# Two thirds of the down projection by Strassen's scheme, one weight pool, and the last 256 tokens written token-major

## The chip, the cores and the metric

The kernel runs on one core of a Trainium2 chip. The metric is the device time of one execution in microseconds (us). A TensorE matmul keeps a 128x128 stationary tile in the array and streams up to 512 columns past it. VectorE (DVE in the profile), ScalarE (ACT), GpSimd (POOL) and SyncE (SP) each run their instructions in their program's order; SP, ACT and POOL also start DMA transfers.

## The reference, cut to what matters

Two layers over 512 tokens of width 1024, all float32. The second half of each layer is the convolutional feed-forward network (FFN), with `D_FF` = 2816; the first half is a mixing block that the change leaves as it is.

```python
def conv_ffn(h, w_up, conv_w, conv_b, w_down):
    up = h @ w_up                                   # 1024 -> 2 x 2816
    s_len = up.shape[1]
    padded = jnp.pad(up, ((0, 0), (CONV_WIDTH - 1, 0), (0, 0)))
    conv = conv_b + padded[:, 0:s_len] * conv_w[0]
    for j in range(1, CONV_WIDTH):
        conv = conv + padded[:, j:j + s_len] * conv_w[j]
    gate, val = jnp.split(conv, 2, axis=-1)
    return (jax.nn.silu(gate) * val) @ w_down       # 2816 -> 1024

    for l in range(DEPTH):
        ...
        x = x + conv_ffn(rms_norm(x, norm2_g[l]), w_up[l], conv_w[l], conv_b[l], w_down[l])
    return rms_norm(x, final_g)
```

## The kernel before

Activations lie with channels on the partitions and the 512 tokens along the free axis: `X` is eight tiles of 128x512. Every large product is taken in three matmuls (`mm3`, line 217): each float32 operand is split into a rounded part (hi, type float32r) and the remainder (lo), and hi·hi, hi·lo and lo·hi are added up in one PSUM bank.

Weights come in slots of 512 KB (128 partitions x 1024 values), 96 per layer, in the order of use. `Weights._emit` (line 81) loads one slot into a raw tile by a DMA on SP's queue, ACT makes the hi tile (line 87) and DVE the lo tile (line 88). There are three pools of five tiles (raw, hi, lo). `get(s)` asks for slots up to `s + LOOK`, that is three ahead.

The FFN (`ffn`, line 591) goes in two halves of 11 channel blocks (`FH`). For each block j two up projections (`proj`, line 223: 8 x 3 matmuls of 512 columns) fill a bank each, one for the gate and one for the value; DVE scales each out of PSUM (line 611), ACT and DVE do the convolution (lines 613 and 617), ACT the SiLU (line 621), DVE the product (line 623), and `split` (line 119) makes the hi and lo tiles of G. After 11 blocks the down projection of the half runs: eight output tiles m, each 11 x 3 matmuls of 512 columns in one bank (`dn`), and one DVE addition into `X[m]` (line 633).

The last half of layer 1 is `finish` (line 640). Its first six output tiles are as above (`fd`); for the last two (`FIN` = 2) the left 256 tokens and then the right 256 tokens are done apart, with matmuls of 256 columns. The squares of `X` are summed, `fin_stats` (line 679) reduces them over the partitions by matmuls (`fss`) and `rsqrt` takes a chain of small DVE and ACT steps; `fin_out` (line 693) spreads the result over the partitions by matmuls with the identity (`frb`) and scales the eight tiles on DVE (line 703) before the output DMAs. The left half's `fin_out` stands among the right half's matmuls, the right half's at the very end.

Within this program text a scheduler (the Tile framework) fixes each engine's order and the semaphores that it waits on, from its own estimates of durations; a tile of a pool can be taken anew only when the last reader of its previous content is done, and that too becomes a wait.

Of the kernel before, what the change touches and what calls it, by code (L numbers as in the profile page):

```python
# [29 lines left out]
NHALF = 2  # L30
FH = FT // NHALF
# [22 lines left out]

class Weights:
    def __init__(self, tc, ctx, wflat):
        self.nc = tc.nc
        self.w = wflat
        self.raw_pool = ctx.enter_context(tc.tile_pool(name="wraw", bufs=5))
        self.hi_pool = ctx.enter_context(tc.tile_pool(name="whi", bufs=LOOK + 2))  # L60
        self.lo_pool = ctx.enter_context(tc.tile_pool(name="wlo", bufs=LOOK + 2))
        self.n = DEPTH * SLOTS_PER_LAYER
        self.next = 0
        self.slots = {}

    def first(self, load_x):
        nc = self.nc
        for s in range(4):
            raw = self.raw_pool.tile([P, 2, T], F32, tag="raw", name=f"wr{s}")
            hi = self.hi_pool.tile([P, 2, T], F32R, tag="hi", name=f"wh{s}")  # L70
            lo = self.lo_pool.tile([P, 2, T], F32R, tag="lo", name=f"wl{s}")
# [28 lines left out]
def trunk(ctx: ExitStack, tc: tile.TileContext, xT, wflat, vec, ws_t, bias_t, bw, rope, dmask, vdec, geps, cnt, sel, out):  # L100
# [3 lines left out]
    up = ctx.enter_context(tc.tile_pool(name="units", bufs=48))  # L104
# [21 lines left out]
    X = []  # L126
# [463 lines left out]

    def ffn(l, nm, nxt):
        base = l * SLOTS_PER_LAYER + 30
        vc = l * LC
        hs, ls = nm.h, nm.l
        s = base
        up_ps = [proj(f"up{l}_0_0", s, hs, ls)]
        nm.stats()
        up_ps.append(proj(f"up{l}_0_1", s + 1, hs, ls))
        nm.spread()
        for hf in range(NHALF):  # L600
            G = []
            for j in range(hf * FH, hf * FH + FH):
                c2 = []
                for which in range(2):
                    n = f"{l}_{j}_{which}"
                    ps = up_ps.pop(0) if up_ps else proj("up" + n, s, hs, ls)
                    s += 1
                    t = which * FT + j
                    w = [vecs[:, vc + C_CW + i * 2 * FT + t : vc + C_CW + i * 2 * FT + t + 1] for i in range(3)]
                    u = U("uu" + n)  # L610
                    nc.vector.tensor_tensor(out=u, in0=ps, in1=nm.bc, op=ALU.mult)  # L611
                    c = U("cc" + n)
                    nc.scalar.activation(  # L613
                        out=c, in_=u, func=AF.Identity, scale=w[2], bias=vecs[:, vc + C_CB + t : vc + C_CB + t + 1]
                    )
                    for d in (1, 2):
                        nc.vector.scalar_tensor_tensor(  # L617
                            out=c[:, d:], in0=u[:, : T - d], scalar=w[2 - d], in1=c[:, d:], op0=ALU.mult, op1=ALU.add
                        )
                    if which == 0:  # L620
                        nc.scalar.activation(out=c, in_=c, func=AF.Silu)  # L621
                    c2.append(c)
                nc.vector.tensor_tensor(out=c2[0], in0=c2[0], in1=c2[1], op=ALU.mult)
                G.append(split(c2[0], f"G{l}_{j}"))
            if nxt is None and hf == NHALF - 1:
                finish(s, G)
                return
            for m in range(KT):
                ps = PS(f"dn{l}_{hf}_{m}")
                for k in range(FH):  # L630
                    i = m * FH + k
                    mm3(ps, W.get(s + i // KT), i % KT, G[k][0], G[k][1], k == 0, k == FH - 1)
                nc.vector.tensor_tensor(out=X[m], in0=X[m], in1=ps, op=ALU.add)  # L633
                if hf == NHALF - 1:
                    nxt.feed(m)
            s += FH
# [202 lines left out]
```

## Time and profile before

| | us |
|---|---|
| median of 3 runs (lowest, highest) | 1140.11 (1140.07, 1140.3) |
| the profiled execution, its own time | 1139.73 |
| its span, first to last instruction | 1138.0 |
| PE busy (matmuls), 5387 instructions | 1128.0 (99%) |
| DVE busy, 1104 instructions | 746.7 (66%) |
| ACT busy, 731 instructions | 525.3 (46%) |

The profiled execution's own time is 1.7 us over its span, for what lies before the first and after the last instruction. Matmuls are pipelined: a 128x512 matmul is shown with some 390 ns, but the next one starts well before it ends, so that what a matmul costs is read from the distance of starts and not from its duration. PEclk is the share of full clock that TensorE was granted.

### The profile page before, as it was taken

What the parts mean: (1) busy time and instruction counts of PE and PEld (TensorE: products, weight loads), DVE (VectorE), ACT (ScalarE), POOL (GpSimd) and SP (SyncE); (2) the same over time, 40 slices, a digit from 0 to 9 for tenths busy, and PEclk for the clock granted to TensorE, in tenths of its full rate; (3) what the DMA queues carried; (4) which work ended last, traced back from release to release, by engine and by line L of the source; (5) the groups of instructions that cost most, each with busy time, mean ns of one, the idle gap of its engine ahead of it and who ended that gap; (6) DMA issues with size and microseconds to landing.
All of it is one profiled execution on the core that took longest, in us unless ns stands there. A gap on an engine that the chain in (4) does not pass through costs nothing.

```text
span 1138.0 us, 13734 instructions
## 1 busy us (share of the span) xinstructions
PE 1128.0 (99%) x5387; PEld 942.3 (83%) x5387; DVE 746.7 (66%) x1104; ACT 525.3 (46%) x731; POOL 27.4 (2%) x71
## 2 busy tenths in 40 slices
PE   9999999999999999999999999999999999999997
PEld 7888888888888888888888898888888888888886
DVE  6998776577753377774448877666777425777534
ACT  7677735444431244444327785534444213444420
POOL 2010000000000000000001000000000000000000
PEclk9999999999999999999999999999999999999999
DMA  9432223232233222333224322222332223222202
GB/s 328 144 117 88 75 75 109 77 111 93 93 96 107 94 93 93 105 99 111 93 93 129 94 77 72 75 95 91 99 105 93 93 95 108 94 93 93 93 1 74
DMA packets 33362, 112.83 MB, mean 99 GB/s; under 512 B 4321, under 2 KB 4497, under 8 KB 33297
## 3 DMA queue, kind: packets, MB, share of 16 engines
q1 hardware_dynamic: 29952, 103.82, 27.4%
q0 software_dynamic: 2480, 6.87, 2.2%
q10 hardware_dynamic: 864, 1.26, 0.3%
q8 instruction: 42, 0.69, 0.3%
q14 instruction: 24, 0.19, 0.0%
HBM read 105.64 MB, written 2.10 MB: 95 GB/s over the span
## 4 chain that ended last, share of the span: by engine, by line
PE 98%; DMA 1%; DVE 0%; SPq 0%; ACT 0%; issue 0%; DVEq 0%
PE up L219 14%; PE up L221 14%; PE up L220 14%; PE dn L219 5%; PE dn L221 5%; PE dn L220 5%; PE o L220 3%; PE o L219 3%; PE o L221 3%; PE fd L219 2%; PE fd L221 2%; PE fd L220 2%; PE q L221 1%; PE k L220 1%; PE k L221 1%; PE q L220 1%
## 5 line engine op out<-in xcount | busy, mean ns | idle before, releaser
L87 ACT CAST wh<-wr 128x1024 fp32r<-128x1024 f32 x188 | 197.9, 1053 | 290.6 <-PE dn L220 104.2
L88 DVE TENSOR_TENSOR wl<-wr,wh 128x1024 fp32r<-128x1024 f32 x188 | 229.8, 1223 | 105.3 <-ACT wh L87 102.4
L617 DVE SCALAR_TENSOR_TENSOR cc<-uu,vecs,cc 128x511 f32<-128x511 f32 (+1 forms) x176 | 131.4, 747 | 5.4 <-ACT cc L613 2.3
L613 ACT ACTIVATE cc<-uu,vecs 128x512 f32<-128x512 f32 x88 | 71.4, 814 | 7.9 <-DVE uu L611 7.7
L621 ACT ACTIVATE cc<-cc 128x512 f32<-128x512 f32 x44 | 27.8, 632 | 78.9 <-DVE cc L617 78.9
L611 DVE TENSOR_TENSOR uu<-up,n_0bc 128x512 f32<-128x512 f32 x44 | 30.2, 687 | 40.9 <-PE up L221 40.9
L611 DVE TENSOR_TENSOR uu<-up,n_1bc 128x512 f32<-128x512 f32 x44 | 30.2, 687 | 40.9 <-PE up L221 40.9
L633 DVE TENSOR_TENSOR x<-x,dn 128x512 f32<-128x512 f32 x24 | 16.5, 686 | 40.9 <-PE dn L221 40.9
L219 PE MATMUL up<-n_0h,wh 128*128 128x512 f32 x88 | 34.6, 393 | 0.0
L219 PE MATMUL up<-n_1h,wh 128*128 128x512 f32 x88 | 34.3, 389 | 0.0
L221 PE MATMUL up<-n_0h,wl 128*128 128x512 f32 x88 | 34.3, 389 | 0.0
L219 PE MATMUL up<-n_2h,wh 128*128 128x512 f32 x88 | 34.3, 389 | 0.0
L220 PE MATMUL up<-n_0l,wh 128*128 128x512 f32 x88 | 34.3, 389 | 0.0
L221 PE MATMUL up<-n_1h,wl 128*128 128x512 f32 x88 | 34.3, 389 | 0.0
L221 PE MATMUL up<-n_2h,wl 128*128 128x512 f32 x88 | 34.2, 389 | 0.0
L219 PE MATMUL up<-n_3h,wh 128*128 128x512 f32 x88 | 34.2, 389 | 0.0
L220 PE MATMUL up<-n_2l,wh 128*128 128x512 f32 x88 | 34.2, 389 | 0.0
L220 PE MATMUL up<-n_3l,wh 128*128 128x512 f32 x88 | 34.2, 389 | 0.0
L221 PE MATMUL up<-n_3h,wl 128*128 128x512 f32 x88 | 34.2, 389 | 0.0
L219 PE MATMUL up<-n_4h,wh 128*128 128x512 f32 x88 | 34.2, 389 | 0.0
L220 PE MATMUL up<-n_4l,wh 128*128 128x512 f32 x88 | 34.2, 389 | 0.0
L221 PE MATMUL up<-n_4h,wl 128*128 128x512 f32 x88 | 34.2, 389 | 0.0
(962 smaller groups left out, 3059.5 us busy)
## 6 DMA issues: line engine op xcount, KB each, us to landing
wr<-in_wflat_dram SPq DMA_DIRECT2D x188, 512.0 KB, 3.5
wr<-in_wflat_dram SPq DMA_DIRECT2D x8, 256.0 KB, 7.2
x<-in_xT_dram SPq DMA_DIRECT2D x8, 256.0 KB, 7.5
qs_0h<-qs_0h POOLq DMA_DIRECT2D x8, 128.0 KB, 2.3
qs_1h<-qs_1h POOLq DMA_DIRECT2D x8, 128.0 KB, 4.5
qs_0l<-qs_0l POOLq DMA_DIRECT2D x8, 128.0 KB, 3.2
qs_1l<-qs_1l POOLq DMA_DIRECT2D x8, 128.0 KB, 3.7
out_dram<-fin ACTq DMA_DIRECT2D x4, 256.0 KB, 2.2
```

What stands on the lines that cost most here:

```text
L87: nc.scalar.copy(hi, src)
L88: nc.vector.tensor_tensor(out=lo, in0=src, in1=hi.bitcast(F32), op=ALU.subtract)
L219: nc.tensor.matmul(ps, hi[:, k, :], xh, start=first, stop=False)
L220: nc.tensor.matmul(ps, hi[:, k, :], xl, start=False, stop=False)
L221: nc.tensor.matmul(ps, lo[:, k, :], xh, start=False, stop=last)
L611: nc.vector.tensor_tensor(out=u, in0=ps, in1=nm.bc, op=ALU.mult)
L613: nc.scalar.activation(out=c, in_=u, func=AF.Identity, scale=w[2], bias=vecs[:, vc + C_CB + t : vc + C_CB + t + 1])
L617: nc.vector.scalar_tensor_tensor(out=c[:, d:], in0=u[:, : T - d], scalar=w[2 - d], in1=c[:, d:], op0=ALU.mult, op1=ALU.add)
L621: nc.scalar.activation(out=c, in_=c, func=AF.Silu)
L633: nc.vector.tensor_tensor(out=X[m], in0=X[m], in1=ps, op=ALU.add)
```

## The change

The 22 channel blocks of the down projection are cut into groups of 8, 8 and 6 (`GROUPS`). The last group is done as before, in `last_down`. For the first two, channel blocks are taken in pairs (ga, gb), output tiles in pairs (m0, m1) and tokens in halves of 256 (LEFT, RIGHT), and each 2x2x2 block of quarter products is done by a scheme of Strassen's kind with seven products in place of eight, every product in three matmuls of 256 columns.

- `combos` makes the seven right operands of a pair of channel blocks: four DVE sums of 256 columns, three splits of 512 columns and one of 256.
- `_pair` makes the seven left operands of a pair of output tiles from two slots: two loads, four DVE sums of 512, and splits of 4.5 slots' halves; the lo part of one slot is made by ACT writing the negated rounded slot (`scale=-1.0`) and a DMA on POOL's queue that adds the raw slot to it (`accum_op`).
- `_plain` with `by_dma` does the same for every second up slot (the value's), in place of DVE's subtraction.
- `down_pair` runs the products in the order 6, 5, 1, 7, 3, 2, 4 in three banks (b, c, a, b, c, a, b) of 256 columns; seven DVE additions follow, one of them over 768 columns. Products 7, 3, 2 and 4 are added on top of what their bank holds.
- All weight tiles share one pool of 16; the pool `units` has 53 tiles in place of 48.
- A group's down projection comes one channel block later than its last up projection (`ahead`).
- The last 256 tokens: ACT scales each `X` tile's right half with the final gain (`scaled`), matmuls with the identity turn it token-major (`turned`), and after the last statistics only four scalings of 128x512 are left, two on DVE and two on ACT, each followed by its output DMA.

```diff
+GROUPS = (8, 8, 6)
+WBUFS = 16
+UBUFS = 53
...
+    def _plain(self, s, by_dma):
+        raw, hi, lo = self.tile(f"wr{s}", F32), self.tile(f"wh{s}"), self.tile(f"wl{s}")
+        nc.sync.dma_start(out=raw, in_=self.w[s].rearrange("p (a t) -> p a t", a=2))
+        nc.scalar.copy(hi, raw)
+        if by_dma:
+            nc.scalar.activation(out=lo, in_=raw, func=AF.Copy, scale=-1.0)
+            nc.gpsimd.dma_start(out=lo, in_=raw, accum_op=ALU.add)
+        else:
+            nc.vector.tensor_tensor(out=lo, in0=raw, in1=hi.bitcast(F32), op=ALU.subtract)
...
+    def _pair(self, s):
+        r0, x1 = self.tile(f"pr{s}", F32), self.tile(f"pq{s}", F32)
+        nc.sync.dma_start(out=x1, in_=self.w[s + 1].rearrange("p (a t) -> p a t", a=2))
+        nc.sync.dma_start(out=r0, in_=self.w[s].rearrange("p (a t) -> p a t", a=2))
+        sums = s12, s34 = [self.tile(f"ps{s}_{i}", F32) for i in range(2)]
+        tt(out=s12[:, 0], in0=x1[:, 0], in1=x1[:, 1], op=ALU.add)
...
+        for i in range(2):
+            h, lo = self.tile(f"pt{s}_{i}"), self.tile(f"pu{s}_{i}")
+            nc.scalar.copy(h, sums[i])
+            tt(out=lo, in0=sums[i], in1=h.bitcast(F32), op=ALU.subtract)
...
+            if i == 0:
+                h0, l0 = self.tile(f"ph{s}"), self.tile(f"pl{s}")
+                nc.scalar.copy(h0, r0)
+                nc.scalar.activation(out=l0, in_=r0, func=AF.Copy, scale=-1.0)
+                nc.gpsimd.dma_start(out=l0, in_=r0, accum_op=ALU.add)
+        r1 = self.tile(f"pv{s}")
+        nc.scalar.copy(r1[:, 0], x1[:, 1])
+        tt(out=r1[:, 1], in0=x1[:, 1], in1=r1[:, 0].bitcast(F32), op=ALU.subtract)
...
+        def down_pair(g, p, s, acts):
+            def part(bank, i, first):
+                if first:
+                    banks[bank] = PS(f"dn{l}_{g}_{p}{bank}")
+                for k, act in enumerate(acts):
+                    mm3(banks[bank][:, :H], wt[i], k, act[i][0], act[i][1], first and k == 0, k == len(acts) - 1, not first)
+                return banks[bank][:, :H]
...
+            add(X[m0][:, RIGHT], part("b", 6, True))
+            add(X[m1][:, RIGHT], part("c", 5, True))
+            q = part("a", 1, True)
+            three = flat[:, m0 * T + H : m0 * T + 4 * H].rearrange("p (a t) -> p a t", a=3)
+            add(three, q.unsqueeze(1).to_broadcast([P, 3, H]))
+            add(X[m1][:, RIGHT], part("b", 7, False))
+            add(X[m0][:, RIGHT], part("c", 3, False))
+            add(X[m0][:, LEFT], part("a", 2, False))
+            add(X[m1][:, LEFT], part("b", 4, False))
...
-        fin_out(1, fin_stats(1, [part, sq]))
...
+        with tc.issue_after(mm.ins):
+            turned(range(2, KT))
+        rt = rsqrt(ss[:, :NB2], NB2, 1.0 / D, "fr1")
+        for hf in range(2):
+            for b in range(NB2):
+                o = U(f"ft{hf}_{b}o")
+                if b:
+                    nc.scalar.activation(out=o, in_=turned_banks[b, hf], func=AF.Identity, scale=rt[:, b : b + 1])
+                else:
+                    nc.vector.tensor_scalar(
```

The scheduler's order at the places that the prediction speaks of follows. Layer 0's first group shows what all four groups of that kind look like.

**The seam, DVE.** Here the last up projection ends and the first down projection begins. Before (block 10 is the last of the half), DVE's order there is:

```order
L617 SCALAR_TENSOR_TENSOR cc_10_0_2896<-uu_10_0_2894,vecs,cc_10_0_2896 128x511
L617 SCALAR_TENSOR_TENSOR cc_10_0_2896<-uu_10_0_2894,vecs,cc_10_0_2896 128x510
L611 TENSOR_TENSOR uu_10_1_2932<-up_10_1_2907,n_0bc 128x512
L88 TENSOR_TENSOR wl_2977<-wr_2974,wh_2976 128x1024
L617 SCALAR_TENSOR_TENSOR cc_10_1_2934<-uu_10_1_2932,vecs,cc_10_1_2934 128x511
L617 SCALAR_TENSOR_TENSOR cc_10_1_2934<-uu_10_1_2932,vecs,cc_10_1_2934 128x510
L623 TENSOR_TENSOR cc_10_0_2896<-cc_10_0_2896,cc_10_1_2934 128x512
L123 TENSOR_TENSOR G_10l<-cc_10_0_2896,G_10h 128x512
L88 TENSOR_TENSOR wl_3009<-wr_3006,wh_3008 128x1024
L633 TENSOR_TENSOR x_118<-x_118,dn_0_0_2943 128x512
```

After, block 8 is the one that runs ahead; `pu_1` and `pv` are the last lo tiles of output pair 1, and `dn_0_0b` is bank b of output pair 0:

```order
L197 TENSOR_TENSOR G_7bl<-cc_7_0_2738,G_7bh 128x512
L710 TENSOR_TENSOR uu_8_0_2847<-up_8_0_2771,n_0bc 128x512
L710 TENSOR_TENSOR uu_8_1_2854<-up_8_1_2822,n_0bc 128x512
L716 SCALAR_TENSOR_TENSOR cc_8_0_2849<-uu_8_0_2847,vecs,cc_8_0_2849 128x511
L716 SCALAR_TENSOR_TENSOR cc_8_0_2849<-uu_8_0_2847,vecs,cc_8_0_2849 128x510
L140 TENSOR_TENSOR pu_1_2816<-ps_1_2801,pt_1_2815 128x1024
L150 TENSOR_TENSOR pv_2819<-pq_2797,pv_2819 128x512
L716 SCALAR_TENSOR_TENSOR cc_8_1_2856<-uu_8_1_2854,vecs,cc_8_1_2856 128x511
L739 TENSOR_TENSOR x<-x,dn_0_0b 128x256
L716 SCALAR_TENSOR_TENSOR cc_8_1_2856<-uu_8_1_2854,vecs,cc_8_1_2856 128x510
L739 TENSOR_TENSOR x<-x,dn_0_0c 128x256
```

The first addition out of a down bank, for which PE waits before it can write that bank again, now stands behind block 8's convolution and the next pair's weights.

**The seam, PE.** After, at the end of product 1 (bank a) and ahead of product 7 (bank b of pair 0 again):

```order
L295 MATMUL dn_0_0a<-G_7a,ph_2699 128x256
L296 MATMUL dn_0_0a<-G_7a,pl_2700 128x256
L294 MATMUL dn_0_1b<-G_1s0h,pt_0_2806 128x256
L295 MATMUL dn_0_1b<-G_1s0l,pt_0_2806 128x256
L296 MATMUL dn_0_1b<-G_1s0h,pu_0_2807 128x256
L294 MATMUL dn_0_1b<-G_3s0h,pt_0_2806 128x256
L295 MATMUL dn_0_1b<-G_3s0l,pt_0_2806 128x256
L296 MATMUL dn_0_1b<-G_3s0h,pu_0_2807 128x256
L294 MATMUL dn_0_1b<-G_5s0h,pt_0_2806 128x256
L294 MATMUL dn_0_0b<-G_1s1h,pt_1_2704 128x256
```

Seven matmuls of pair 1's first product (`dn_0_1b`) were moved ahead of product 7; before, a bank of the down projection is written once and the matmuls stand in the order of the text.

**The up projections, ACT.** Before, from block 2 to block 4 of layer 0:

```order
L613 ACTIVATE cc_2_1_2294<-uu_2_1_2292,vecs 128x512
L122 CAST G_2h<-cc_2_0_2256 128x512
L87 CAST wh_2385<-wr_2383 128x1024
L613 ACTIVATE cc_3_0_2336<-uu_3_0_2334,vecs 128x512
L621 ACTIVATE cc_3_0_2336<-cc_3_0_2336 128x512
L87 CAST wh_2423<-wr_2421 128x1024
L613 ACTIVATE cc_3_1_2374<-uu_3_1_2372,vecs 128x512
L122 CAST G_3h<-cc_3_0_2336 128x512
```

After, from the end of block 3 to block 5; `wl_2578` is the negated slot 45 to which POOL's DMA then adds, and `wh_2609` (slot 46) is put into the tile that held the raw slot 45, so that it waits for that DMA:

```order
L119 ACTIVATE wl_2578<-wr_2576 128x1024
L196 CAST G_3s1h<-G_3t_2384 128x512
L196 CAST G_3bh<-cc_3_0_2368 128x512
L712 ACTIVATE cc_4_0_2466<-uu_4_0_2464,vecs 128x512
L117 CAST wh_2609<-wr_2608 128x1024
L720 ACTIVATE cc_4_0_2466<-cc_4_0_2466 128x512
L712 ACTIVATE cc_4_1_2473<-uu_4_1_2471,vecs 128x512
L117 CAST wh_2654<-wr_2653 128x1024
L119 ACTIVATE wl_2655<-wr_2653 128x1024
L712 ACTIVATE cc_5_0_2543<-uu_5_0_2541,vecs 128x512
```

ACT has one more pass over every second slot, and one of its casts waits for a DMA's landing.

## Rows read from the trace of the kernel before


**Rows 1.** Page parts 1, 2: busy us, share, instructions; granted clock by slices.

```profile
PE 1128.0 (99%) x5387; PEld 942.3 (83%) x5387; DVE 746.7 (66%) x1104; ACT 525.3 (46%) x731; POOL 27.4 (2%) x71
...
PEclk9999999999999999999999999999999999999999
```

**Rows 2.** The page, part 4: the chain that ended last, by engine.

```profile
PE 98%; DMA 1%; DVE 0%; SPq 0%; ACT 0%; issue 0%; DVEq 0%
```

**Rows 3.** Waits of PE: who waited for whom, us in total, times, longest.

```profile
PE frb L696 <- DVE fr1r L169: 1.3, 1, 1.3
PE fss L684 <- ACT fq L650: 0.6, 1, 0.6
```

**Rows 4.** Timeline of PE, 512 columns: start us, us, line, what; 15 matmuls apart.

```profile
560.03 0.39 PE L219 MATMUL dn<-G_13h,wh 128*128 128x512 f32 x1
...
563.43 0.39 PE L219 MATMUL dn<-G_18h,wh 128*128 128x512 f32 x1
```

**Rows 5.** Timeline of PE, 256 columns in the last half; 52 matmuls apart.

```profile
1110.66 0.28 PE L220 MATMUL fd<-G_11l,wh 128*128 128x256 f32 x1
...
1116.90 0.28 PE L221 MATMUL fd<-G_17h,wl 128*128 128x256 f32 x1
```

**Rows 6.** Groups of DVE by line and shape: count, busy us, mean ns, idle before.

```profile
L88 DVE TENSOR_TENSOR wl<-wr,wh 128x1024 fp32r<-128x1024 f32 x188 | 229.8, 1223 | 105.3 <-ACT wh L87 102.4
...
L617 DVE SCALAR_TENSOR_TENSOR cc<-uu,vecs,cc 128x511 f32<-128x511 f32 x88 | 65.6, 745 | 2.3 <-ACT cc L613 2.3
...
L633 DVE TENSOR_TENSOR x<-x,dn 128x512 f32<-128x512 f32 x24 | 16.5, 686 | 40.9 <-PE dn L221 40.9
```

**Rows 7.** Groups of ACT by line and shape.

```profile
L87 ACT CAST wh<-wr 128x1024 fp32r<-128x1024 f32 x188 | 197.9, 1053 | 290.6 <-PE dn L220 104.2 <-PE up L220 66.8 <-PE o L220 39.8
L613 ACT ACTIVATE cc<-uu,vecs 128x512 f32<-128x512 f32 x88 | 71.4, 814 | 7.9 <-DVE uu L611 7.7
L621 ACT ACTIVATE cc<-cc 128x512 f32<-128x512 f32 x44 | 27.8, 632 | 78.9 <-DVE cc L617 78.9
```

**Rows 8.** The page, parts 3 and 6: DMA queue load, and transfers from issue to landing.

```profile
q1 hardware_dynamic: 29952, 103.82, 27.4%
...
wr<-in_wflat_dram SPq DMA_DIRECT2D x188, 512.0 KB, 3.5
...
qs_0h<-qs_0h POOLq DMA_DIRECT2D x8, 128.0 KB, 2.3
```

**Rows 9.** All DMA issues: the one 512 KB transfer on POOL's queue.

```profile
dmt<-in_dmask_dram POOLq DMA_DIRECT2D x1, 512.0 KB, 7.4
```

**Rows 10.** Instructions of tile qs_0h on POOL: ns min/median/max of the issuing instruction.

```profile
L341 POOL DMA_DIRECT2D qs_0h<-qs_0h x8: 516/516/530, 43.2 to 661.0; - x8
```

**Rows 11.** Busy us by stretch: PE, PEld, DVE, ACT, POOL, clock, DMA share, GB/s.

```profile
30.00:284.00 254.00, 254.00 (x1295) 213.65 (x1294) 191.55 (x317) 145.48 (x220) 10.98 (x28) 1.00 0.30 98
```

**Rows 12.** Timeline of DVE at layer 0's last seam, idle time in brackets.

```profile
507.37 1.23 DVE L88 TENSOR_TENSOR wl<-wr,wh 128x1024 fp32r<-128x1024 f32 x1 [0.17 <-ACT wh L87]
...
511.45 0.69 DVE L123 TENSOR_TENSOR G_21l<-cc,G_21h 128x512 fp32r<-128x512 f32 x1 [0.69 <-ACT G_21h L122]
512.81 1.23 DVE L88 TENSOR_TENSOR wl<-wr,wh 128x1024 fp32r<-128x1024 f32 x1 [0.66 <-ACT wh L87]
```

**Rows 13.** Timeline of all engines at the end of the program.

```profile
1123.51 0.42 DVE L648 TENSOR_TENSOR x<-x,fd 128x256 f32<-128x256 f32 x1 [1.37 <-PE fd L221]
...
1123.95 3.22 DVE L703 SCALAR_TENSOR_TENSOR fin<-x,vecs,frb 128x256 f32<-128x256 f32 x8
...
1128.36 0.42 ACT L650 ACTIVATE fq<-x 128x256 f32<-128x256 f32 x1 [3.98 <-DVE x L648]
1128.83 0.52 PEld L684 LDWEIGHTS fss<-ones,fq 128*128 128x128 f32 x4 [0.71 <-ACT fq L650]
...
1130.77 0.52 PEld L696 LDWEIGHTS frb<-ident,fr1r 128*128 128x128 f32 x4 [1.42 <-DVE fr1r L169]
...
1131.52 3.22 DVE L703 SCALAR_TENSOR_TENSOR fin<-x,vecs,frb 128x256 f32<-128x256 f32 x8 [0.80 <-PE frb L696]
```

More of the change, by code (lines that the diff above doesn't have):

```diff
@@ L124, in split @@
         return hi, lo
-    X = []
+    XB = cp.tile([P, KT, T], F32, name="x")
+    X = [XB[:, k] for k in range(KT)]
     vecs = cp.tile([P, NV], F32, name="vecs")
@@ L591, in ffn @@
     def ffn(l, nm, nxt):
-        base = l * SLOTS_PER_LAYER + 30
+        s = l * SLOTS_PER_LAYER + 30
         vc = l * LC
         hs, ls = nm.h, nm.l
[L595 to L614, printed above, removed]
-                    )
[L616 to L636, printed above, removed]
@@ new lines, in ffn @@
+        G, pend = {}, None
+        top = 0
+        for what, i in _ffn_plan():
+            if what == "up":
+                g = next(x for x in range(len(GROUPS)) if i < sum(GROUPS[: x + 1]))
+                o = up(i, s)
+                s += 2
+                if g == len(GROUPS) - 1:
+                    G.setdefault(g, []).append(split(o, f"G{l}_{i}"))
+                elif (i - sum(GROUPS[:g])) % 2 == 0:
+                    pend = o
+                else:
+                    G.setdefault(g, []).append(combos(f"G{l}_{i}", pend, o))
+            elif i < len(GROUPS) - 1:
+                for p in range(KT // 2):
+                    down_pair(i, p, s + 2 * p, G[i])
+                G.pop(i)
+                s += KT
+            else:
+                last_down(l, s, G[i], nxt)
@@ L648, in down @@
[L648 removed]
+                i = m * n + k
+                mm3(ps, W.get(s + i // KT), i % KT, G[k][0][:, c], G[k][1][:, c], k == 0, k == n - 1)
+            return ps
+        whole = slice(0, T)
+        for m in range(2):
+            partial(m, whole, 0, n - 2)
+        def down(m, c, hook=None):
+            ps = partial(m, c, n - 2 if m < 2 else 0, n, hook)
+            nc.vector.tensor_tensor(out=X[m][:, c], in0=X[m][:, c], in1=ps, op=ALU.add)
@@ L649, in down, with square @@
+        if nxt is not None:
+            for m in range(KT):
+                down(m, whole)
+                nxt.feed(m)
+            return
+        def square(m, c):
             sq = U(f"fq{m}_{c.start}")[:, : c.stop - c.start]
@@ L651, in down @@
             return sq
-        total = down(0, slice(0, T), T)
+        down(0, whole)
+        total = square(0, whole)
         warm = sp.tile([P, 1], F32, tag="warm", name="warm_f")
@@ L656, in finish, with scaled, turned @@
         for m in range(1, KT - FIN):
-            sq = down(m, slice(0, T), T)
-            nc.vector.tensor_tensor(out=total, in0=total, in1=sq, op=ALU.add)
+            down(m, whole)
+            nc.vector.tensor_tensor(out=total, in0=total, in1=square(m, whole), op=ALU.add)
         r = {}
+        turn = {}
+        def scaled(k):
+            xg = U(f"xg{k}")[:, :H]
+            nc.scalar.activation(
+                out=xg, in_=X[k][:, H:], func=AF.Identity, scale=vecs[:, C_FG + k : C_FG + k + 1]
+            )
+            turn[k] = xg
+        def turned(ks):
+            for k in ks:
+                for b in range(NB2):
+                    if (b, k // 4) not in turned_banks:
+                        turned_banks[b, k // 4] = PS(f"ft{b}_{k // 4}")
+                    nc.tensor.matmul(
+                        turned_banks[b, k // 4][:, k % 4 * P : k % 4 * P + P],
+                        turn[k][:, b * P : (b + 1) * P],
+                        ident,
+                        start=True,
+                        stop=True,
+                    )
+        turned_banks = {}
         for th in range(2):
```

218 lines of the change are left out of this document (172 added, 46 removed).

## The prediction

> **What bounds the kernel now.** I read the busy shares first, then the chain of work that ended last, then the waits of PE. PE is busy for 1128.0 of 1138.0 us at full granted clock in every slice [rows 1], the chain that set the end is 98% PE [rows 2], and in mid-program PE waits for nobody: its listed waits are 1.3 and 0.6 us in the final statistics [rows 3]. So before the last addition the time is the number of matmuls by their pace, and DVE (66%) and ACT (46%) have room. A gain must come from fewer matmul microseconds; a loss must come from making PE wait, which it does not do now.
>
> The pace is read from distances of starts. With 512 columns, 15 matmuls take 3.40 us, 226.7 ns each [rows 4]. With 256 columns, 52 take 6.24 us, 120.0 ns each [rows 5]: a half matmul costs 53% of a whole one.
>
> **Part 1, fewer matmuls.** Two output tiles by eight channel blocks cost 2x8x3 = 48 matmuls of 512 columns, 10.88 us. The seven products cost 7x4x3 = 84 of 256 columns, 10.08 us. Each such pair saves 0.80 us, and there are 4 pairs x 2 groups x 2 layers = 16: -12.80. Of the scheme's 12.5% only 7.4% is left, because half matmuls are dear. In layer 1's last group the two tiles done by halves shrink from 11 to 6 channel blocks, so 72 half matmuls are left of 132; each costs 120.0 - 226.7 / 2 = 6.65 ns more than half a whole one: -0.40. Sum for PE -13.2. Of it, the right half of the last tile (33 matmuls before, 18 now, 1.8 us) lies after the addition at 1123.51 (call it point a), so -11.4 falls before a.
>
> The Trainium skill, "TensorE: Matmul & The Clock Gate", section "Back-to-back issue gap", puts starts N / 2.4 GHz plus some 2.5 ns apart, 216 and 109 ns. By it a pair would go from 10.36 to 9.17 us, sixteen would save 19.0, and the time would be near 1126.3. The measured 226.7 and 120.0 [rows 4, 5] disagree, and decide.
>
> **Part 2, the tail.** Before, a to the end is 14.5 us (1138.0 - 1123.51). After, the left half's spreading has only 6 matmuls (0.72 us) to cover its statistics chain, which took 1.94 us from `fss` to `frb` at the end [rows 13]; its eight scalings (3.22 us) then start near a+1.6 and end at a+4.8. ACT meanwhile does squares and eight final-gain scalings of 256 columns (0.42 each [rows 13]), held up by two DMA issues that wait for the scalings, and reaches the last one near a+6.9. Statistics 1.94 give a+8.5 to 8.9, two scalings of 512 columns on DVE (0.69 each by the additions out of PSUM [rows 6]) a+9.9 to 10.3, and from the last scaling to the end it is 3.26 as before (1131.52 + 3.22 = 1134.74 to 1138.0): a+13.1 to 13.9. Gain 0.6 to 1.4; I take 1.0. With -11.4, the sum without new waits is **-12.4**.
>
> **Part 3, vector work beside the products.** A weight pair costs DVE four sums and one half remainder of 512 columns (5 x 0.69) and two remainders of 1024 (2 x 1.22), 5.9 us; its seven additions cost 6 x 0.42 and one of 768 columns, an estimate of 0.95 between the rows of 512 and 1024 [rows 6], 3.5 us. Together 9.4 of the 10.08 us that PE takes: hidden, but with 0.7 spare, where before a stretch of the whole kernel had a quarter of DVE free (191.55 of 254 us busy [rows 11]). A group's last pair prepares nothing for itself, so over a group it is 34 of 40 us. In the up projections two blocks take PE 96 x 0.2267 = 21.76 us; DVE needed 16.35 (4 x 0.69 out of PSUM, 8 x 0.745, 4 x 0.69 for product and split, 4 x 1.22) and now 16.7: two 1.22 fewer, four sums and one remainder of 0.42 and one of 0.69 more. ACT needed some 10 (4 x 1.05, 4 x 0.81, 2 x 0.63, two casts of 512 columns at an estimated half of 1.05) and now 13: two more passes of 1.05 and one and a half more casts [rows 6, 7]. No engine passes PE on average. If this cover is gone, see rival C.
>
> **Part 4, the accumulating DMA.** The trace has no such transfer. Landing times near it: 2.3 for 128 KB on POOL, 3.5 for 512 KB on SP [rows 8], 7.4 for the one of 512 KB on POOL, in the crowded start [rows 9]. It must read its target too: 512 KB occupy the 16 engines for 1.57 us (27.4% of 1138 us by 0.524 / 103.82 MB [rows 8]). Estimate D = 3.5 + 1.57 = 5.1 us, ends 2.3 and 7.4; SP's row is the nearest since size and load agree. Who waits: the next rounded up slot goes into the raw tile that the transfer reads, so that ACT's cast waits for it, and behind that cast ACT's queue holds the next convolution and SiLU. Per two blocks ACT has two such waits, with some 2 of its 13 us running beneath them: 2D + 11.0 us, within 21.76 while D is under 5.4. So it costs nothing at 5.1, and by a margin of 0.3.
>
> The Trainium skill, "SBUF — State Buffer", section "SBUF: two separate sides", warns that POOL cannot write the descriptors of its DMAs while DVE runs certain fast modes. In the trace POOL's issuing instruction takes 516 to 530 ns each time [rows 10] while DVE is 75% busy [rows 11]: no hold-up is seen for small transfers, and none of 512 KB there tells.
>
> **Part 5, the seam.** PE's product 7 (bank b again) waits for DVE's addition out of bank b, and DVE has block 8's two convolutions, the last combinations, two pairs' weights and that addition in one queue. From the end of the last needed up projection to that addition I add up 10 x 0.69 + 6 x 0.42 + 5 x 0.75 + 2 x 1.22 = 15.6 us of DVE work [rows 6, 13]. PE has 10.88 of up projection, 4.32 of products 6, 5, 1 and 0.84 of seven matmuls moved ahead: 16.0. So the seam is free if DVE never waits in it. It does wait: before, it lost 0.17 + 0.69 + 0.66 = 1.5 us to ACT at the same place [rows 12], and now it also waits there for the transfer into `pl`. Bounds: 0 and, walking each queue at D = 5.2 with every wait in full, 2.8 us. I take 1.2 for each of four seams (the row's 1.5 less the spare 0.4 is 1.1, and a little for the new transfer): **+4.8**. Pairs' additions behind waits in mid-group I set at nothing, by the 0.7 spare.
>
> WBUFS, UBUFS and the longer lead of the up projections move no work of their own; PE reaches the loads later than before, and SP's queue is at 27.4% [rows 8].
>
> **The sum.** 1139.73 - 12.4 + 4.8 = 1132.1 on the profiled execution, which stands 0.38 below the median: **1132.5**. Seams of 0.5 to 2.5 us each give 1129.7 to 1137.7.
>
> **The rivals.** *B, the seams are free*: DVE gets its data in time, as it does wherever it has slack. For it: 15.6 against 16.0 on paper; against: the 1.5 us of row waits. 1139.73 - 12.4 + 0.4 = 1127.7.
>
> *A, the transfer is slow, and the kernel slower*: above D = 5.4 ACT falls behind by 2D - 10.8 us per two blocks, about three times in an up phase; I count half of the backlog at the seam, as the weights' lead covers some. The seams eat the 12.4 when each costs 3.1, that is at D = 6.0. At D = 7.0 they cost 1.2 + 0.5 x 3 x 3.2 = 6.0, four of them 24, and the time is 1151.7. For it: 7.4 in the only row of that size on that queue; against: that row is of the start, with other loads around it. The descriptor hold-up would do it as well: put off by one DVE instruction of 1.22 us, D = 6.3, the seams 3.9 each, 1143.3. That is the mechanism of the SBUF page's warning of the Trainium skill above.
>
> *C, the change doesn't do what it says*: in the Strassen stage DVE, at 9.4 of 10.08 us and with waits of 1.5 us as in the seam, sets the pace. If three pairs of four take 10.88 as before, 0.75 x 12.8 = 9.6 is lost: 1132.5 + 9.6 - 4.8 (the seams' wait would be the same one) to 1137.3 to 1142. For it: seven additions by one engine that also prepares weights; against: three banks and a lead of one pair.
>
> **How the numbers follow.** Forecast 0.43, B 0.21, C 0.13, A 0.22, the page's faster pace 0.01. A measurement of this kernel tells about 0.2% from no change: faster is below 1137.8, slower above 1142.4. The forecast, B and the page's pace are faster (0.65); C lies within for 0.09 and 0.02 on either side; of A, D between 5.4 and 6 is faster (0.04), the rest slower (0.18). Faster 0.71, same 0.09, slower 0.20. The range starts below B, at 1126.5 (a tail gain of 1.4 and some more), and goes up through C and most of A, to 1149; past it lies D near 6.8 and more.
>
> **What would show it.** Starts of 256-column matmuls 120 ns apart in `dn`, a pair 10.08 us from first to last start (part 1). At the four seams, idle time of PE before product 7 that names DVE's addition, 0.5 to 2.5 us (part 5); none would be B. The accumulating DMA lands 5 us after its issue, and ACT's waits for it are short; 6 and more, with waits of several us that end on that queue, is A. PE idle inside groups at banks a to c, put down to `pu` or `x` of DVE, is C. From a to the end 13 to 14 us (part 2). The forecast is wrong above all if D is not near 5.1, since the margin there is 0.3 us.

## The result

| | median of the runs (lowest, highest), us | ratio to before, 95% interval |
|---|---|---|
| before, in the same comparison | 1140.18 (1140.07, 1140.3) | |
| after | 1168.89 (1167.17, 1174.07) | 1.0259 (1.0226 to 1.0293) |

The changed kernel is 2.6% slower, 36 us above the prediction of 1132.5 and 20 above its range. The profiled execution has a span of 1165.4 us. Its page, parts 1 and 2 (busy time and granted clock), the chain that ended last by engine, and the longest waits of PE (who waited for whom, us in total, times, longest), where [rows 1 to 3] stood:

```profile
PE 1134.3 (97%) x5961; PEld 970.1 (83%) x5961; DVE 810.9 (70%) x1326; ACT 613.8 (53%) x865; POOL 80.2 (7%) x131
...
PEclk9998999999999999999999989999999999999999
...
PE 67%; DVE 13%; issue 8%; DMA 7%; ACT 4%; POOL 0%; ACTq 0%; DVEq 0%; POOLq 0%; SPq 0%
```

```profile
PE dn_0b L294 <- ACT G_7s0h L196: 6.8, 2, 3.9
PE sc L443 <- DVE S_0l L197: 5.2, 2, 3.0
PE dn_0b L294 <- DVE x L739: 3.4, 4, 1.3
PE dn_2b L294 <- DVE x L739: 2.7, 2, 1.6
```

PE has 574 more instructions and 6 us more busy time, the clock is below full in two slices, and the chain is 67% PE where it was 98%. PE now waits, in two places: at the score matmuls of the mixing block (`sc`), and at the seams (`dn`). Cutting the span at PE's first statistics matmul of each stage and at point a, the addition into `X[6]`'s right half (1150.22 in after), shows where the time went; the last column is e12, with e14 the fastest kernel of the experiments, for later use:

| stage, us | before | after | e12 |
|---|---|---|---|
| start | 25.7 | 26.5 | 25.7 |
| mixing, layer 0 | 184.9 | 191.9 | 184.9 |
| FFN, layer 0 | 374.5 | 380.5 | 368.9 |
| mixing, layer 1 | 184.8 | 192.0 | 184.8 |
| FFN, layer 1, to point a | 353.5 | 359.3 | 349.2 |
| point a to the end | 14.5 | 15.2 | 15.3 |
| span | 1138.0 | 1165.4 | 1128.8 |

**The pace was as forecast.** Timeline of PE in a Strassen pair of layer 0, 42 matmuls of 256 columns apart (start, us, line, what), as [rows 5] was read:

```profile
450.07 0.28 PE L294 MATMUL dn_0b<-G_9s0h,pt 128*128 128x256 f32 x1
...
455.10 0.28 PE L294 MATMUL dn_1b<-G_13s0h,pt 128*128 128x256 f32 x1
```

5.03 us for 42 are 119.8 ns each. So was the landing time. DMA issues of the page, part 6 (count, KB each, median us from issue to landing), beside [rows 8, 9], and, for `wl`, POOL's instruction (ns, lowest, median, highest) and the landing times:

```profile
wl<-wr POOLq DMA_DIRECT2D x44, 512.0 KB, 5.1
...
pl<-pr POOLq DMA_DIRECT2D x16, 512.0 KB, 4.8
```

```profile
L120 POOL DMA_DIRECT2D wl<-wr x44: 860/872/937, 190.8 to 1094.4; - x44
...
DMA to landing us min/median/max: 4.5/5.1/9.9
```

D was estimated at 5.1 us and is 5.1 and 4.8 in the median, with a spread: `wl` lands between 4.5 and 9.9 us, `pl` between 4.5 and 7.5, and 21 of the 60 are above the 5.4 at which the prediction's margin ends. While the longest was under way (932.1 to 942.0) the 16 DMA engines were 90% busy with it and other loads; in one of 4.55 us (from 284.55), with no load beside it, 61%. POOL's instruction takes 860 to 937 ns wherever it stands. So the hold-up of descriptors that the Trainium skill, "SBUF — State Buffer", section "SBUF: two separate sides", warns of does not show here. The plain loads were not slowed in the median (`wr` 3.6 us, 3.5 before).

**The mixing block.** The change does not touch its text, yet each loses 7 us. DVE's timeline in layer 0, of before and then of after, at the same remainders of the scores (`S_0l`):

```profile
102.89 0.69 DVE L123 TENSOR_TENSOR S_0l<-sc,S_0h 128x512 fp32r<-128x512 f32 x1
103.50 0.55 DVE L123 TENSOR_TENSOR S_1l<-sc,S_1h 128x384 fp32r<-128x384 f32 x1
104.15 1.23 DVE L88 TENSOR_TENSOR wl<-wr,wh 128x1024 fp32r<-128x1024 f32 x1
```

```profile
106.23 0.30 DVE L448 TENSOR_TENSOR sc<-sc,dmt 128x128 f32<-128x128 f32 x1
106.56 1.22 DVE L122 TENSOR_TENSOR wl<-wr,wh 128x1024 fp32r<-128x1024 f32 x1
107.71 0.68 DVE L197 TENSOR_TENSOR S_0l<-sc,S_0h 128x512 fp32r<-128x512 f32 x1
```

Before, the weight's remainder (`wl`) stood behind `S_1l`; now it stands ahead of `S_0l`, and the chain ahead of it is late as well (the same `S_0l` starts 4.8 us later, while the kernel was only 0.7 late at 100 us). PE can write the next scores only when `S_0l` has been made out of the bank. Timeline of PE there, and then the busy time by stretch (PE, PEld, DVE, ACT, POOL, then the granted clock):

```profile
108.44 0.58 PE L443 MATMUL sc<-qs_1h,ks 128*128 128x256 f32 x1 [2.95 <-DVE S_0l L197]
...
113.41 0.41 PE L323 MATMUL va<-wh,n_0h 128*128 128x256 f32 x1
113.62 0.41 PE L324 MATMUL va<-wl,n_0h 128*128 128x256 f32 x1
```

```profile
105.00:110.00 5.00, 2.05 (x9) 1.53 (x8) 4.72 (x8) 3.49 (x6) 1.55 (x3) 0.84 0.55 159
110.00:115.00 5.00, 5.00 (x24) 4.90 (x23) 2.58 (x7) 3.81 (x6) 0.00 (x0) 0.50 0.00 0
```

A wait of 2.95 us is followed by 5 us at half the granted clock: the two matmuls of 256 columns start 0.21 us apart where 0.12 is normal. In layer 1 the wait is 2.25.

**The seams.** PE at layer 0's first seam:

```profile
314.66 0.28 PE L296 MATMUL dn_0b<-G_5s0h,pu 128*128 128x256 f32 x1
318.87 0.38 PE L294 MATMUL dn_0b<-G_7s0h,pt 128*128 128x256 f32 x1 [3.93 <-ACT G_7s0h L196]
319.60 0.38 PE L295 MATMUL dn_0b<-G_7s0l,pt 128*128 128x256 f32 x1 [0.34 <-DVE G_7s0l L197]
```

The products wait 3.9 us for `G_7s0h`, the last combination, where before PE waited for nothing and DVE stood idle for 1.5 us [rows 12]; later ones wait for additions into `X`. At the four seams in order, gaps of PE's starts over 226.7 and 120.0 ns come to 7.1, 2.0, 6.4 and 2.3 us, and slower starts behind them to some 3.5 more.

### The profile page after: what moved, and what is told of

Read it like the earlier page. It is cut to its first block, busy times and chain, and to the rows that moved or that the text cites. A ratio compares the mean times of both kernels' runs of the same rounds, so it can differ in the third digit from the quotient of the medians.

```text
span 1165.4 us, 15463 instructions
## 1 busy us (share of the span) xinstructions
PE 1134.3 (97%) x5961; PEld 970.1 (83%) x5961; DVE 810.9 (70%) x1326; ACT 613.8 (53%) x865; POOL 80.2 (7%) x131
## 4 chain that ended last, share of the span: by engine, by line
PE 67%; DVE 13%; issue 8%; DMA 7%; ACT 4%; POOL 0%; ACTq 0%; DVEq 0%; POOLq 0%; SPq 0%
PE up L294 8%; PE up L296 8%; PE up L295 8%; PE o L296 2%; PE o L295 2%; PE o L294 2%; DVE cc L716 2%; PE fd L295 2%; PE fd L296 2%; PE fd L294 2%; DMA wl<-wr 2%; DMA pr<-in_wflat_dram 2%; DMA pl<-pr 1%; DMA wr<-in_wflat_dram 1%; DVE pu L140 1%
## 5 line engine op out<-in xcount | busy, mean ns | idle before, releaser
L117 ACT CAST wh<-wr 128x1024 fp32r<-128x1024 f32 x156 | 162.5, 1044 | 124.1 <-DMA wr<-in_wflat_dram 89.7
L122 DVE TENSOR_TENSOR wl<-wr,wh 128x1024 fp32r<-128x1024 f32 x112 | 136.7, 1221 | 63.0 <-ACT wh L117 33.0
L120 POOL DMA_DIRECT2D wl<-wr x44 | 38.4, 873 | 450.5 <-ACT wl L119 345.7
L139 ACT CAST pt<-ps 128x1024 fp32r<-128x1024 f32 x32 | 33.3, 1042 | 58.2 <-DVE ps L133 26.6
L119 ACT ACTIVATE wl<-wr 128x1024 fp32r<-128x1024 f32 x44 | 46.3, 1052 | 0.0
L140 DVE TENSOR_TENSOR pu<-ps,pt 128x1024 fp32r<-128x1024 f32 x32 | 39.0, 1220 | 4.5 <-DMA pl<-pr 3.1
L295 PE MATMUL up<-n_7l,wh 128*128 128x512 f32 x88 | 34.3, 390 | 0.0
L295 PE MATMUL up<-n_1l,wh 128*128 128x512 f32 x88 | 34.2, 389 | 0.0
L296 PE MATMUL up<-n_7h,wl 128*128 128x512 f32 x88 | 34.2, 389 | 0.0
```

What stands on the lines that cost most here:

```text
L117: nc.scalar.copy(hi, raw)
L119: nc.scalar.activation(out=lo, in_=raw, func=AF.Copy, scale=-1.0)
L120: nc.gpsimd.dma_start(out=lo, in_=raw, accum_op=ALU.add)
L122: nc.vector.tensor_tensor(out=lo, in0=raw, in1=hi.bitcast(F32), op=ALU.subtract)
L139: nc.scalar.copy(h, sums[i])
L140: tt(out=lo, in0=sums[i], in1=h.bitcast(F32), op=ALU.subtract)
```

## The experiments

The theories. **P**: the one pool changes the scheduler's order in the mixing blocks. **W**: DVE's work alone fills the seams. **A** (rival A of the prediction), later **R** and **T**: what fills them is the waiting for accumulating transfers to land. The kernel before, timed beside each group of experiments, took 1139.9 to 1140.2 us, so that medians of different groups can be set side by side. The scheduler orders every kernel anew, and DVE's order in e2 and e3 differs from after's in many places that the edit does not touch: a difference between two kernels holds work, waits and order together.

### e1: the one pool alone

```diff
+WBUFS = 16
...
-        self.raw_pool = ctx.enter_context(tc.tile_pool(name="wraw", bufs=5))
-        self.hi_pool = ctx.enter_context(tc.tile_pool(name="whi", bufs=LOOK + 2))
-        self.lo_pool = ctx.enter_context(tc.tile_pool(name="wlo", bufs=LOOK + 2))
+        self.pool = ctx.enter_context(tc.tile_pool(name="w", bufs=WBUFS))
...
```

> The kernel before with one edit: its three weight pools of five tiles become one pool of 16. Theory P (the shared pool changes the scheduler's order on DVE and ACT in the mixing blocks, and PE then waits there): each mixing block loses the 7 us that it loses in the changed kernel, 1140.2 + 14 = about 1154, with a PE wait of some 3 us at the score matmuls of layer 0 and a granted clock near 0.5 behind it. Rival (the mixing block is late for another reason, the larger units pool, the order of the rest of the program or the POOL transfers): within 0.3% of 1140.2.

Measured: 1157.11 us, ratio 1.0148 (1.0133 to 1.0163): 17 us slower. PE's longest wait and DVE's order at the score remainders:

```profile
PE sc L367 <- DVE S_0l L122: 5.2, 2, 3.0
```

```profile
107.58 1.23 DVE L87 TENSOR_TENSOR wl<-wr,wh 128x1024 fp32r<-128x1024 f32 x1
108.72 0.68 DVE L122 TENSOR_TENSOR S_0l<-sc,S_0h 128x512 fp32r<-128x512 f32 x1
```

The same wait of 5.2 us in two, behind the same `wl`; its mixing blocks take 193.0 and 190.5 us, 8.0 and 5.6 more than before; the start is 1.9 longer. P holds. In e1 no line of the mixing block or of the FFN differs from the kernel before.

### e2: no accumulating transfers

```diff
-            nc.gpsimd.dma_start(out=lo, in_=raw, accum_op=ALU.add)
...
-                nc.gpsimd.dma_start(out=l0, in_=r0, accum_op=ALU.add)
```

> The changed kernel without the accumulating transfers: the lo tiles that they would complete hold only the negated raw slot, so the result differs; everything else is kept. Theory W (at the seams DVE has more work than time): only DVE's waits for these transfers go, about 1.1 us at the first seam of each layer, 1164 to 1168. Rival A of the prediction (the transfers' landing time holds ACT and DVE up): the four seams' stalls of some 18 us and the low clock behind them go, 1145 to 1150.

Measured: 1147.69 us, ratio 1.0069 (1.0046 to 1.0091), 21 us less than after. No wait of PE at `dn` is left in its list. W in its first form falls: the waits of DVE that name a transfer were 1.1 and 2.0 us in after, one at the first seam of each layer, and taking the transfers away gave back all of the seams. In e2 nobody does the work of the transfers; e13 closes that gap.

### e3 and e4: less DVE work, more lead

```diff
-                for d in (1, 2):
+                for d in (1,):
```

> The changed kernel with one of the two shifted taps of the convolution left out, so that DVE does one instruction of 0.75 us less for each of 88 projections and the result differs. Theory W: DVE's backlog at a seam falls by at least the four taps of two blocks, 3 us, more where it builds up over several blocks; the two seams of 7 us fall under 3, the two of 2 us vanish, with the clock's share 14 to 18 us less, 1151 to 1155. Rival A (transfers): DVE waits as long for them as before, 1165 to 1169.

```diff
-        ahead = 1 if g < len(GROUPS) - 1 else 0
+        ahead = 2 if g < len(GROUPS) - 1 else 0
```

> The changed kernel with two channel blocks of the next group, not one, done ahead of a group's down projection. Theory W: PE gets 10.9 us more of work ahead of the seam and DVE 8.4 us more, so that some 2.5 us of each seam's stall go, with the clock's share 10 us in all: 1157 to 1161. Rival A: the transfers get 10.9 us more as well, and the seams vanish: 1148 to 1152.

Measured: 1173.06 and 1182.13 us; neither theory's numbers. Busy time of e3 (page, part 1), and PE's longest waits at the seams in e3 and then in e4:

```profile
PE 1135.7 (97%) x5961; PEld 973.0 (83%) x5961; DVE 750.9 (64%) x1238; ACT 615.3 (53%) x865; POOL 80.0 (7%) x131
```

```profile
PE dn_0b L294 <- DVE x L739: 6.7, 2, 4.6
```

```profile
PE dn_0b L294 <- DVE x L739: 15.0, 2, 8.3
...
PE dn_1b L296 <- DVE pu L140: 3.7, 2, 3.4
```

e3's DVE is busy 750.9 us, 60 less than in after, and PE's waits at `dn` come to 16.8 us (15.1 in after): less DVE work alone does not free the seams, though the order changed with it. In e4 the longest single wait grew to 8.3 us; why more lead makes it worse was not followed.

### What a transfer holds up

With these two the question was where 5.1 us turn into 7 at a seam. Waits of DMA issues (SP's queue) and of ACT in after:

```profile
SPq L130 <- DMA wl<-wr: 23.8, 2, 12.9
```

```profile
ACT wh L117 <- DMA wl<-wr: 22.0, 9, 7.1
```

The second of the first pair's two loads (`pr`, line 130) waits up to 12.9 us for the transfer of an up slot. In the one pool it is given the raw tile of slot 47, the last up slot, which the transfer still reads. DVE then waits for that load, and later for the pair's own transfer (start, us, line, what, idle before):

```profile
292.61 0.69 DVE L133 TENSOR_TENSOR ps<-ps,pr 128x512 f32<-128x512 f32 x1 [1.31 <-DMA pr<-in_wflat_dram]
...
304.98 1.22 DVE L140 TENSOR_TENSOR pu<-ps,pt 128x1024 fp32r<-128x1024 f32 x1 [1.11 <-DMA pl<-pr]
```

So the work on the pair's sums falls to DVE in the same stretch as the last combinations, and all of it arrives late at the seam.

### e5 to e8

e5: the pool cut into four, 5 + 5 + 5 + 1 tiles.

```diff
-        self.pool = ctx.enter_context(tc.tile_pool(name="w", bufs=WBUFS))
+        self.pools = {k: ctx.enter_context(tc.tile_pool(name="w" + k, bufs=n)) for k, n in (("raw", 5), ("hi", 5), ("lo", 5), ("v", 1))}
...
-        return self.pool.tile([P, 2, T], dt, tag="w", name=name)
+        k = {"wr": "raw", "pr": "raw", "pq": "raw", "ps": "raw", "wh": "hi", "pt": "hi", "ph": "hi", "pv": "v"}.get(name[:2], "lo")
+        return self.pools[k].tile([P, 2, T], dt, tag=k, name=name)
```

> The changed kernel with its one weight pool of 16 tiles cut up: five tiles for what is loaded and for sums, five for rounded parts, five for remainders, one for the last operand of a pair. The order in the mixing blocks is then that of before. Theory P: the mixing blocks take 185 us again, some 14 us less. Theory R (at a layer's first seam the load of the first pair waits for the raw tile of the last up slot, which the accumulating transfer still reads; DVE gets the pair's sums late): the load no longer waits for that tile, and the 7 us seams fall under 3, some 9 us less. Together 1143 to 1149. Theory W (DVE's work alone fills the seams): 1153 to 1156.

e6: the last value slot ahead of each Strassen group made by DVE (kind "s", not "d"). e7: each pair's `l0` by DVE in place of negation and transfer. e8: the last 256 tokens as before.

```diff
-                jobs += [(s, "s", 1), (s + 1, "d", 1)]
+                jobs += [(s, "s", 1), (s + 1, "s" if i in (GROUPS[0], GROUPS[0] + GROUPS[1]) else "d", 1)]     # e6
...
-                nc.scalar.activation(out=l0, in_=r0, func=AF.Copy, scale=-1.0)
-                nc.gpsimd.dma_start(out=l0, in_=r0, accum_op=ALU.add)
+                tt(out=l0, in0=r0, in1=h0.bitcast(F32), op=ALU.subtract)            # e7
...
+        fin_out(1, fin_stats(1, [part, sq]))                                        # e8
```

> The changed kernel in which the last value slot ahead of each Strassen group (4 of 44) gets its remainder from DVE's subtraction and not from the transfer; one pool as in the changed kernel. Theory R: the first pair's load does not wait for a transfer, is issued some 5 us earlier or more, and the first seam of each layer falls from 7 us to under 3: 1157 to 1162. Theory W: DVE has 1.2 us more to do there: 1168 to 1172.

> The changed kernel in which the remainder that each pair gets from a transfer comes from DVE's subtraction, 1.22 us for each of 16 pairs; the transfers of the up slots stay. Theory R: the load of the first pair is as late as before and DVE has 10.6 us of work for 10.08 us of products: 1169 to 1178. Rival A' (what holds the seams up is the pair's own transfer, for which DVE waits 1.1 us): 1158 to 1163.

> The changed kernel with the end of the program as before (spreading by matmuls, eight scalings of 256 columns). All theories: from the addition of the seventh tile's right half to the end 14.5 to 15.5 us, where the changed kernel took 15.2; the total 1166 to 1170.

Measured: e5 1145.51, e6 1172.87, e7 1164.01, e8 1173.26 (one run). In e5 the mixing blocks take 184.9 us each: P again. Its seams shrank but stayed, some 13 us over four; the two of 7 us became 3.9 and 4.7, where R had said under 3, so that the total fell into the range of P and R with one of its two parts off. e6 lies outside R's range, just above W's, and refutes my narrow form of R: SP's queue shows that the pair's load then waited for DVE's subtraction of the same slot, so it was little better off.

```profile
SPq L130 <- DVE wl L122: 15.8, 2, 8.3
```

e7 lies between R and A'. The second seam of each layer is free of waits although DVE does more, the first is not: the pair's own transfer lies behind the second, and the up slots' transfers are left for the first. e8 tells nothing in time beside a spread of 7 us between runs of after; its end from point a (1156.73) takes 14.8 us.

### e9 to e12: four pools, and which transfers

All have e5's pools and the old end. e9: pairs by DVE, up slots by transfer. e10: as e9 with the token-major end. e11: up slots by DVE, pairs by transfer. e12: no transfer.

```diff
-                jobs += [(s, "s", 1), (s + 1, "d", 1)]
+                jobs += [(s, "s", 1), (s + 1, "s", 1)]                              # e11, e12
...
-                nc.scalar.activation(out=l0, in_=r0, func=AF.Copy, scale=-1.0)
-                nc.gpsimd.dma_start(out=l0, in_=r0, accum_op=ALU.add)
+                tt(out=l0, in0=r0, in1=h0.bitcast(F32), op=ALU.subtract)            # e9, e10, e12
```

> The kernel of four pools (e5) with two more edits: the pairs' remainders come from DVE's subtraction, and the end of the program is that of the kernel before. Theory T (the seams that are left in e5, 13 us with the clock, come from the pairs' transfers, which hold pool tiles and make DVE wait): the seams vanish, the end takes 14.8 us for 17.6: 1145.5 - 13 - 2.8 = about 1130, faster than the kernel before. Theory W (DVE's work sets the pace once it has 10.6 us for 10.08 us of products): the gain of the scheme is lost in the pairs, 1140 to 1148.

> As e9 with the changed kernel's token-major end. Theory T: 1132 to 1134, the difference to e9 being the end (15.2 to 17.6 us for 14.8, by the granted clock in it). Theory W: 1142 to 1151.

> As e9, but the up slots' remainders come from DVE and the pairs' from the transfers. Theory T: the seams of e5 stay, 1141 to 1145. Rival A'' (it is the up slots' transfers that make the seams): 1129 to 1133. Theory W: DVE has 19.1 us of 21.8 us per two blocks in place of 16.7, seams longer than in e5, 1145 to 1155.

> As e9 without any accumulating transfer: all remainders come from DVE, which then has 19.1 of 21.8 us per two blocks and 10.6 us per pair. Theory T: as e9 within 3 us, 1129 to 1133, if DVE's spare time lasts. Theory W: 1145 to 1160.

Measured: e9 1149.60, e10 1153.93 (runs from 1149.7 to 1154.2), e11 1138.54 (ratio 0.9987, 0.9977 to 0.9997), **e12 1130.58** (ratio 0.9915, 0.9901 to 0.9930). T's numbers for e9 and e10 were 20 us too low: it blamed the pairs' transfers alone. W's ranges ended 2 and 3 us below the two, so that it is not their times but the waits, and e12, that speak against W. DVE's waits in e9 show that the up slots' transfers hold the tile of a sum (`ps`), and that the pair's load comes late:

```profile
DVE ps L133 <- DMA wl<-wr: 10.3, 4, 2.6
...
DVE ps L134 <- DMA pr<-in_wflat_dram: 5.3, 4, 1.6
```

e11 lies between T and A'': each kind of transfer costs something. With no transfer, PE's only wait at a Strassen product is 0.2 us, and DVE is busier than in any other kernel here (876.5 us; 746.7 before):

```profile
PE 1116.4 (99%) x5933; PEld 958.5 (85%) x5933; DVE 876.5 (78%) x1392; ACT 558.0 (49%) x795; POOL 27.5 (2%) x71
```

```profile
PE dn_2b L294 <- DVE x L739: 0.2, 1, 0.2
```

### e13 and e14: transfers and pool apart

e13 is the changed kernel with its one pool and its end, and DVE making every remainder. e14 is e12 with the token-major end. In e13 the two edits of e12 above stand on the changed kernel.

> The changed kernel with its one pool and its token-major end, in which DVE's subtraction makes every remainder and no accumulating transfer is left. DVE then has 19.1 of 21.8 us per two blocks and 10.6 us per pair. Theory T (the seams come from waits for the transfers' landing, not from the amount of DVE work): the seams vanish as in the run without the transfers, 1144 to 1150, the rest above 1130 being the mixing blocks of the one pool (14 to 17 us). Theory W (DVE's work fills the seams, and the run without transfers was only fast because nobody did that work): 1165 to 1180.

> The kernel without transfers and with four pools (e12), but with the changed kernel's token-major end. If that end costs what the traces show, 15.2 us at full granted clock and 17.5 us where the clock falls while PE waits in it, against 15.3 in e12: 1130.5 to 1133.5. If it gained the 1.0 us of the prediction: 1129.5.

Measured: e13 1145.85 (ratio 1.0053, 1.0038 to 1.0068), e14 1130.42 (0.9913, 0.9896 to 0.9930). With the token-major end, the two parts stand apart:

| median, us | with transfers | without |
|---|---|---|
| one pool | 1168.89 (after) | 1145.85 (e13) |
| four pools | 1145.51 (e5) | 1130.42 (e14) |

The transfers cost 23 us with one pool and 15 with four; the one pool costs 23 with transfers and 15 without, of which the mixing blocks make 14 (191.8 and 192.1 us in e13, 184.9 and 184.9 in e14). The ends of the four profiled executions took 15.2, 14.9, 17.6 and 17.6 us (after, e13, e5, e14), by the granted clock in them, so that these differences hold to some 3 us. Busy time of the 30 us ahead of the first seam, after and then e13 (PE, PEld, DVE, ACT, POOL), and the issue of the same load in both; the products begin at 313.7 and 313.4:

```profile
284.00:314.00 30.00, 30.00 (x135) 24.88 (x134) 24.61 (x40) 14.96 (x22) 1.74 (x2) 1.00 0.37 88
```

```profile
284.00:314.00 30.00, 30.00 (x137) 24.94 (x136) 28.39 (x46) 15.79 (x22) 0.00 (x0) 1.00 0.11 36
```

```profile
289.16 0.33 SPq L130 DMA_DIRECT2D pr<-in_wflat_dram  x1
```

```profile
276.75 0.33 SPq L130 DMA_DIRECT2D pr<-in_wflat_dram  x1
```

DVE did 3.8 us more in e13 and had no arrears, and the load went out 12 us earlier. It is not work that DVE lacked time for but data. In both kernels the load waits for a reader of the raw tile of slot 47, in after the transfer, in e13 DVE's subtraction. Most of the 12 us had been lost before, on ACT; its casts of slots 46 and 47 in after (behind the negation of slot 45, which starts a transfer), and of slot 47 in e13:

```profile
273.13 1.05 ACT L119 ACTIVATE wl<-wr 128x1024 fp32r<-128x1024 f32 x1
...
279.86 1.05 ACT L117 CAST wh<-wr 128x1024 fp32r<-128x1024 f32 x1 [2.39 <-DMA wl<-wr]
...
282.25 1.05 ACT L117 CAST wh<-wr 128x1024 fp32r<-128x1024 f32 x1
```

```profile
273.66 1.03 ACT L117 CAST wh<-wr 128x1024 fp32r<-128x1024 f32 x1
```

ACT reached slot 47 8.6 us later; the negation and the transfer that follow, in place of a subtraction, make the other 3.8.

## Why the prediction was wrong

**Part 1** was right: 119.8 ns measured for 120.0. In e12 the first Strassen group takes 40.9 us for the 40.3 worked out. Up to point a, e12's stages gain 5.6 + 4.3 = 9.9 us for the forecast 11.4, the scheme's gain nearly whole.

**The weight pool** is the first step that failed. "WBUFS, UBUFS and the longer lead of the up projections move no work of their own" dismissed the pool in a sentence: e1 measures 17 us for it. A tile of a pool becomes free by a reader that the scheduler estimates; another pool gives other times, and the scheduler writes another order for all engines, in code that the diff does not name. The prediction compared the orders in the FFN only. UBUFS and the longer lead stand in e12 and e14 as well, and no loss shows there.

**Part 4** had the size right (a median of 5.1) and the chain wrong, at two points. It asked who waits for the transfer on ACT, and found 2D + 11.0 = 21.2 within 21.76 us. In layer 0's first up projections the casts of slots 38, 40, 42, 44 and 46, each of which waited for the transfer ahead of it, start from 231.89 to 279.86 us, 12.0 apart: ACT took 24.0 us for two blocks and fell behind PE, as rival A describes, at a D that part 4 had called free. The sum had left out that ACT waits for DVE's results between the transfers (1.96 us ahead of the cast at 272.60). And it did not ask who else gets the tile that the transfer reads: the next pair's load, for up to 12.9 us. "So it costs nothing at 5.1" measures 23 us between after and e13. The first of these casts, the last being the one at 279.86 above:

```profile
231.89 1.05 ACT L117 CAST wh<-wr 128x1024 fp32r<-128x1024 f32 x1 [7.13 <-DMA wl<-wr]
```

**Part 5** gave 4.8 us for the seams; 17.8 of gaps and some 3.5 of slower starts were measured, of which waits of 4.2 us at the third pair (`dn_2`) had been set at nothing. Its sum of 15.6 us supposed that DVE enters the stretch without arrears. In after, DVE scaled block 7's first projection at 307.3 us; PE had made it by 297.4 (three projections of 5.44 us ahead of the products at 313.7). The spare 0.4 us was the difference of two sums and no bound. The 34 us that part 3 gives DVE for a group do not follow from its terms (4 x 9.4 less 5.9 is 31.7); nothing rests on them.

**Part 2**, the end, came to 15.2 us for 13.1 to 13.9 (14.5 before, [rows 13]). Two terms were short: the second pair of scalings waited for the last of 24 turning matmuls, which the sum left out, and from the last scaling to the end it took 4.2 us, not 3.26. Timeline of the end of after and of e14, where the same matmuls ran at half the granted clock:

```profile
1157.51 2.92 PE L827 MATMUL ft<-ident,xg 128*128 128x128 f32 x24
...
1160.47 0.69 ACT L878 ACTIVATE ft_1o<-ft,fr1r 128x512 f32<-128x512 f32 x1 [0.76 <-PE ft L827]
```

```profile
1121.93 5.47 PE L827 MATMUL ft<-ident,xg 128*128 128x128 f32 x24
...
1127.43 0.69 ACT L878 ACTIVATE ft_1o<-ft,fr1r 128x512 f32<-128x512 f32 x1 [2.73 <-PE ft L827]
```

e14's profile is of the slowest of its four executions (1133.59 us; the others 1130.05 to 1130.51), so its end need not be the usual one. The medians of e12 and e14 (1130.58 and 1130.42) do not tell the two ends apart.

**The rivals.** A named the right cause, the transfers, and one link of its chain, ACT's casts; its point of decision, D = 6.0, was wrong: at 5.1 the transfers already cost 15 to 23 us, more than the whole gain of 12.4. C fell: DVE does more in e12 to e14 than in after, and no product waits over 0.7 us for it. B, free seams at 1127.7, is what e12 and e14 come near to, once the pool and the transfers are gone; both beat the kernel before by 0.9%.

## What to carry to other kernels

A change to a pool is a change to the order of the whole program: compare the orders everywhere, in the code that the diff leaves alone too. For an operation that is moved from an engine to a DMA, ask how long the DMA holds its source and target tiles and who is next to use them; 1.2 us of DVE's time were saved here at the price of 5 us in which a tile was not free and an instruction of ACT. An engine at 95% of a stretch can keep pace, and one at 82% can be late, when its data come late.

## What was not expected of the hardware

A wait of PE costs more than its length: behind 2.95 us of waiting the granted clock was 0.50 (1.2 GHz) for the 5 us that follow, and in the end of e14 0.50 over 24 matmuls, 5.47 us for 2.92. The Trainium skill, "TensorE: Matmul & The Clock Gate", section "What's actually happening", says that throttling is the default state and activity releases it; the traces agree in that the clock fell behind PE's waits and came back under matmuls (0.98 from 115 to 120 us). What decides it they do not show: the end of after, with the same waits of PE as that of e14, kept the full clock (2.92 us). Before had no such stretch in mid-program, where its PE never waited.

POOL's instruction for a 512 KB transfer takes 872 ns where one of 128 KB took 516 [rows 10].
